# Byte-counted attention steps, flat convolution and spread state loads in a decoder trunk on one core

## The chip, the core and the metric

The kernel runs on one core of one Trainium2 chip. The metric is the device time of one execution in microseconds; lower is better. A core has TensorE (PE, with its weight loads as PEld), VectorE (DVE), ScalarE (ACT), GpSimd (POOL) and SyncE (SP), which issues nearly all transfers of this kernel.

## The reference

One inference step of a decoder layer over 256 prompt tokens and 8 x 8 sample tokens (320 columns in all), width 2048, all in float32:

```
x += 0.5 * SwiGLU_a(RMSNorm(x))            # 2048 -> 2 x 5632 -> 2048
x += TokenMix(RMSNorm(x))
x += 0.5 * SwiGLU_b(RMSNorm(x))
y  = RMSNorm(x)
```

TokenMix has one combined input projection (2048 to 11,272 columns) whose columns feed two branches. Branch A is an mLSTM with 4 heads: its q and k pass a causal convolution of width 4 over time and a SiLU; a matrix state C (256 x 256 for each head, and for each of the 8 sample sequences) is read for the sample tokens and updated. Branch B is dilated causal attention with 8 heads: the prompt attends to itself, and each sample sequence attends to 2048 old keys and values at distances 0, d, 2d, ... for three patterns, near (128 and 512 back) and far (every 16th of 2048). The branches are projected back (w_pm, w_pa), gated, added and passed through w_out. Outputs are y, the new keys and values, the new states and the last three rows before the convolution.

```
y = b + sum_i xx[:, i:i+T] * w[i]                 # causal convolution, i = 0..3
num = wgt @ v + sc * (q @ C0)                     # mLSTM, C0 of each sample sequence
C_new = sT * C0 + e * k^T v
p = softmax over old keys, new keys, three patterns; o = p @ v
```

## The kernel before

Everything hangs on one long stream of projection work on TensorE. Each weight matrix is cut into chunks of 512 x 256 numbers (512 KB). A chunk is loaded into a `raw` buffer (5 of them), rounded by ScalarE into `hi` (L236) and by VectorE into the remainder `lo = raw - hi` (L113, the call of the metered VectorE; 3 buffers each), and multiplied on TensorE (L144) in 24 matmuls of 320 columns: hi and lo of the weights against hi and lo of the activations. These results go to the PSUM tiles named `fg`. All other matmuls and transposes go to the four PSUM buffers named `bg`.

`run_job` (L282) is the planner: it walks the chunks in order, and all other work is written as Python generators that are advanced between chunks, so that their instructions lie between the matmuls of the stream. At each chunk it runs, in this order: transfers and steps that were put off by a number of chunks (`later`, `run_later`), the evacuation of the job before, the rounding of the chunk two ahead (`split_upto`), small steps put off in the same way (`soon`), then on even ticks the lists `even` and `slow`, on odd ticks the list `odd`, then the evacuations that have several steps (`every`), and last the list `fill`, as long as VectorE has room by the planner's own count (`Metered`, L103: every VectorE instruction is charged 0.16 us and 0.00104 us an element, against 3.2 us a chunk plus what extra matmuls take). At its end it loads weights as far as seven chunks ahead (`load_upto`, L202). A turn of a generator in `slow` or `odd` is thus two chunks.

Since SyncE issues all transfers in program order (`dma`, L135), a transfer that waits for a buffer or for data holds up all that stand behind it. TensorE, too, takes its instructions in program order.

The stage that matters is the combined input projection, 45 jobs. Beside it run:

- `sample_attention` (L643), in `slow`: the attention of the sample tokens to old keys and values, in 16 units of one sequence and four heads (u). It first loads near keys (`nk`) and far keys (`fk`), waits until the second job of keys is there (`M["ak"]`, L756), and starts `far_work` (L700), in `fill`: scores of the far keys on VectorE and ScalarE. Each unit takes four turns, every fourth unit five (L880): products with the old values of the unit before (`pv`, L809, tiles `vt` and `pf`) and scores of this unit; then the loads of this unit's five old-value tiles of 512 KB (`values`, L804, 5 buffers) and the next near keys, one a chunk; then probabilities.
- `combine` (L883): the transposes of four units' results, the tile `hsS`; the last one loads the attention result back as `ar`, which the branch projection w_pa needs.
- `prompt_attention` (L582), in `even`: it scales its probabilities on VectorE (L605).
- `qk_evac` (L995): the convolution. Prompt and sample columns of an evacuated projection stand in `pre` (3 columns of padding, 256 of the prompt, 8 x 11 of the samples). For each of two row blocks and four taps there are two instructions, of 256 and of 64 columns, into `y`, a tile of a ring of 19 buffers; the first tap is on ScalarE (L1018), three on VectorE; then tanh, `(tanh + 1) * y` on VectorE, and the store to `qk_d`.
- `mlstm` (L1057), in `odd`: for each head, `load_head`, `prep`, `front`, `update`, and two products of the queries with the states (`retrieve`, L1165; 16 matmuls on four tiles `C` of 256 KB). `load_c` (L1085) asks for the next four tiles at once, in five buffers. Its calls stand here (L1260 and on), a `yield` ending a turn:

```
for i in range(2):
    yield
    retrieve(h, i, CC.pop(2 * h + i))
    ...
    yield
    if i == 0:
        make_qm(h, 1)
    load_cc(2 * h + i + 1)
    ...
    yield
```

A state product is the first work of its chunk on TensorE; the matmuls of that chunk stand behind it.

Of the kernel before, what the change touches and what calls it, by code (L numbers as in the profile page):

```python
# [18 lines left out]
SEQ = 256  # L19
# [37 lines left out]
def _consts():  # L57
    c = {}
    p = np.arange(128)
    c["ident"] = np.eye(128, dtype=np.float32)  # L60
    mk = np.full((4, 4, 8, SCOLS), NEG, np.float32)
    for i in range(4):
        for t in range(8):
            mk[:, i, t, 0:128] = _logmult(512 + t - 128 * i - p)
            if i == 0:
                mk[:, i, t, 128:136] = _logmult(t - np.arange(8))
                mk[:, i, t, 136] = 0.0
            mk[:, i, t, 137] = 0.0
    mk = mk.reshape(128, SCOLS)
    c["msk_s"] = mk  # L70
    c["msk_p"] = _logmult(128 + p[:, None] - np.arange(256)[None])
    q = np.arange(32)
    bd = (p[:, None] // 32 == q[None] // 8).astype(np.float32)
    b8, t8 = np.divmod(np.arange(64), 8)
    kt_, bg_, bt_ = p // 64, (p // 32) % 2, p % 32
    sels = (bg_[:, None] * 32 + bt_[:, None] == np.arange(64)[None]).astype(np.float32)
    s4 = np.stack([np.arange(4), 3 - np.arange(4)], axis=1)
    qmask = np.tile((s4[:, :, None] == q // 8).astype(np.float32).reshape(1, 256), (128, 1))
    cm = np.full((128, 448), BIG, np.float32)
    cm[:, 0:256] = np.where(p[:, None] <= np.arange(256)[None], 0.0, BIG)  # L80
    cm[:, 256:384] = np.where(p[:, None] <= p[None], 0.0, BIG)
    s = np.arange(64)
    ok = (s[:, None] // 8 == s[None] // 8) & (s[:, None] <= s[None])
    cm[64:, 384:448] = np.where(ok, 0.0, BIG)
# [12 lines left out]


M_BD, M_SELS, M_QM, M_CM, M_TS, M_LD = 0, 32, 96, 352, 800, 832
MIXW = 833  # L100


class Metered:  # L103
# [3 lines left out]
    def __getattr__(self, name):  # L107
        fn = getattr(self.engine, name)

        def call(*a, **k):  # L110
            n = math.prod((a[1] if name == "tensor_reduce" else a[0]).shape[1:])
            self.load += 0.16 + n * (0.0066 if name == "reciprocal" else 0.00104)
            return fn(*a, **k)  # L113

        return call
# [8 lines left out]
def decoder_kernel(tc, I, O, K):  # L124
# [8 lines left out]
    es.enter_context(tc.manual_schedule())  # L133

    def dma(out, in_):  # L135
        nc.sync.dma_start(out, in_)  # L136

# [144 lines left out]
    def run_job(job):  # L282
# [4 lines left out]
        for n, (ci, k0, nk) in enumerate(cs):  # L287
            V.next_chunk(CHUNK_US + extra[0])
            extra[0] = 0.0
            run_later()  # L290
# [8 lines left out]
            if tick[0] % 2 == 0:  # L299
                step(even)  # L300
                step(slow)
            else:
# [46 lines left out]
    n0T = cp.tile([128, 64], F32, name="n0T")  # L349
    mskp = cp.tile([128, 256], F32, name="mskp")  # L350
    sTb = cp.tile([128, 32], F32, name="sTb")
# [230 lines left out]
    def prompt_attention(p):  # L582
        tb = m2_tile("tp")
        tbv = tb.rearrange("p (h c) -> p h c", h=2)
        dma(tb, I["bias_p"][p])
        G.tensor_tensor(tbv, tbv, bcast(mskp, 2), op=OP.add)
        q, k, v = QT[p], KT_[p], VP[p]
# [17 lines left out]
        def scale(m):  # L605
            s, ns = S_[m], N_[m]
            V.reciprocal(ns[:, 2:4], ns[:, 2:4])
            V.tensor_scalar(s[:, 0:128], s[:, 0:128], ns[:, 2:3], None, op0=OP.mult)
            V.tensor_scalar(s[:, 128:384], s[:, 128:384], ns[:, 3:4], None, op0=OP.mult)

# [32 lines left out]
    def sample_attention():  # L643
# [109 lines left out]
        for n in range(FKB):  # L753
            load_far(n)
            yield
        while M["ak"] < 1:  # L756
            yield
        q4 = make_q4(0)
        load_qr(0)
        yield  # L760
        load_qr(1)
        fill.append(far_work())

# [78 lines left out]
        for u in range(17):  # L842
# [23 lines left out]
            s = soft(u, sp)  # L866
            values(u, 5, 0, 1)
            later(lambda u=u: load_near(2 * u + NKB), 1)
# [4 lines left out]
            later(lambda u=u: load_near(2 * u + 1 + NKB), 1)  # L873
            values(u, 2, 3, 4)
            yield
# [3 lines left out]
            yield  # L879
            if u % 4 == 3:  # L880
                yield

# [112 lines left out]
    def qk_evac(ps, j):  # L995
# [11 lines left out]
        yield  # L1007
        y = t_tile(F32, "y")
        for m in range(2):
# [3 lines left out]
            for i in range(4):  # L1013
                w = gv[:, G_CW + 16 * i + kt:G_CW + 16 * i + kt + 1]
                for o, x in ((y[:, m, 0:SEQ], pre[:, m, i:i + SEQ]),
                             (y[:, m, SEQ:NT].rearrange("p (b t) -> p b t", b=8), pres[:, m, :, i:i + 8])):
                    if i == 0:
                        S.activation(o, x, AF.Identity, scale=w, bias=gv[:, G_CB + kt:G_CB + kt + 1])  # L1018
                    else:
                        V.scalar_tensor_tensor(o, x, w, o, op0=OP.mult, op1=OP.add)  # L1020
        yield
        e = pret[:, 0:2 * NT].rearrange("p (m c) -> p m c", m=2)
        S.activation(e, y, AF.Tanh)
        M["tanh"] = True
        yield
        V.scalar_tensor_tensor(e, e, 1.0, y, op0=OP.add, op1=OP.mult)
        if j >= 4:
# [29 lines left out]
    def mlstm():  # L1057
        mix = M["mix"]
        qmk = mix[:, M_QM:M_QM + 256].rearrange("p (a n c) -> p a n c", a=4, n=2)
        cm = mix[:, M_CM:M_CM + 448]  # L1060
        sels = mix[:, M_SELS:M_SELS + 64]
# [23 lines left out]
        def load_c(h, i):  # L1085
            c = []
            for b in (2 * i, 7 - 2 * i, 2 * i + 1, 6 - 2 * i):
                c.append(mxt([128, 512], "C", 5, "C"))
                load_state(c[-1], b, h)
            return c  # L1090

# [7 lines left out]
        def prep(h):  # L1099
            d = H[h]  # L1100
            q, k, re = d["q"], d["k"], d["re"]
            z = m2_tile("z")
            for j, (c0, c1, t0) in enumerate(((0, 256, 0), (256, 384, 128), (384, 448, 256))):
                V.scalar_tensor_tensor(z[:, c0:c1], re[:, 0, t0:t0 + c1 - c0], aeT[:, j, h:h + 1], cm[:, c0:c1],
                                       op0=OP.subtract, op1=OP.max)
# [151 lines left out]
        for h in range(4):  # L1257
            for i in range(2):
# [8 lines left out]
                if i == 1 and h < 3:  # L1267
                    while M["qk"] < 2 * (h + 2):
                        yield
                    load_head(h + 1)  # L1270
                yield
            yield
            numer(h)
# [26 lines left out]
    def mixer_open():  # L1300
# [10 lines left out]
        M["mix"] = c([128, MIXW], "mixc")  # L1311
        dma(M["mix"], K["mix"])
        M["cvn"] = c([128, 16, 27], "cvn")
        M["bif"] = c([36, 1], "bif")
# [316 lines left out]
    def init_tables():  # L1631
# [5 lines left out]
        dma(msk, K["msk_s"])  # L1637
        dma(mskp, K["msk_p"])
        dma(convst, I["conv_t"].rearrange("p (k c) -> p k c", k=16))
# [141 lines left out]
```

## Time and profile before

| | us |
|---|---|
| median of 3 runs (2677.07 to 2678.86) | 2678.45 |
| profiled execution, its own time | 2678.66 |
| its span in the profile | 2676.9 |
| TensorE busy in the span | 2652.1 |
| VectorE busy | 1516.8 |
| ScalarE busy | 1128.1 |

The granted TensorE clock is full throughout. Rows of the profile name the engine, the line of the kernel, the operation and the tiles (out<-in); a line of a helper such as L113, L136 or L144 serves many callers, so the tiles tell what it is. The list of waits says which engine sat idle for whom: total us, times, longest. The chain of waits follows back what ended last. SPq is SyncE's queue of transfers. In the timeline a row gives the start in us from the start of the span, the length in us and how many instructions were merged into it.

### The profile page before, as it was taken

Reading aid. Unit: us, or ns where it says so; the run is one execution under the profiler, and the core shown is the slowest. Engines: PE = TensorE matmul, PEld = TensorE weight load, DVE = VectorE, ACT = ScalarE, POOL = GpSimd, SP = SyncE. Lnnn points to the kernel's source line nnn. Section 1 sums busy time; section 2 is a strip of 40 time slices with the busy share of each in tenths; the row PEclk is TensorE's granted clock in tenths of the full one; section 3 lists DMA queues with packets and bytes.
Section 4 is the critical chain, followed back from the end, with each engine's and each line's share of the span. In section 5 each row is a group of like instructions: output and inputs, shape, how many; then the busy total and the mean of one; then the engine's idle time right before and its main releaser. Section 6 shows DMA issues by size and latency. Waiting matters only on the chain.

```text
span 2676.9 us, 50899 instructions
## 1 busy us (share of the span) xinstructions
PE 2652.1 (99%) x21286; PEld 2632.1 (98%) x21286; DVE 1516.8 (57%) x1994; ACT 1128.1 (42%) x1865; POOL 146.7 (5%) x167
## 2 busy tenths in 40 slices
PE   9999999999999999999999999999999999999998
PEld 9999999999999999999999999999999999999997
DVE  6444444444446577777766656655555555554445
ACT  6333333333334445555544444444333333333344
POOL 0000000000000000011211000000000000000000
PEclk9999999999999999999999999999999999999999
DMA  6554544445546779899999876665556556555543
GB/s 232 163 168 159 164 160 163 158 155 165 169 158 187 239 221 320 282 346 334 338 364 347 320 244 223 199 204 191 193 193 192 190 185 193 187 173 172 160 151 130
DMA packets 198596, 568.48 MB, mean 212 GB/s; under 512 B 23249, under 2 KB 61273, under 8 KB 198365
## 3 DMA queue, kind: packets, MB, share of 16 engines
q1 hardware_dynamic: 197644, 563.91, 63.4%
q8 instruction: 166, 2.72, 0.4%
q10 hardware_dynamic: 720, 1.31, 0.1%
q14 instruction: 66, 0.53, 0.1%
HBM read 533.41 MB, written 31.73 MB: 211 GB/s over the span
## 4 chain that ended last, share of the span: by engine, by line
PE 93%; DMA 4%; DVE 1%; ACT 1%; issue 1%; SPq 0%; DVEq 0%; ACTq 0%
PE fg L144 89%; PE bg L144 3%; DMA vt<-in_old_v_dram 2%; DVE lo L113 0%; PE bg L357 0%; ACT hi L236 0%; DMA qr<-qt_d 0%; DMA C<-in_state_C_dram 0%; DMA k<-qk_d 0%; DMA raw<-in_w_in_dram 0%; DMA fk<-in_far_k_dram 0%; SPq L136 0%; DVE x L113 0%; DMA raw<-in_w_ffa_in_dram 0%; DMA scb<-sc_d 0%
## 5 line engine op out<-in xcount | busy, mean ns | idle before, releaser
L113 DVE TENSOR_TENSOR lo<-raw,hi 128x1024 fp32r<-128x1024 f32 (+1 forms) x788 | 964.2, 1229 | 855.9 <-ACT hi L236 838.7
L144 PE MATMUL fg<-xh,hi 128*128 128x320 f32 x4232 | 1273.0, 302 | 1.7 <-ACT hi L236 0.9
L144 PE MATMUL fg<-xh,lo 128*128 128x320 f32 x4232 | 1262.2, 299 | 1.2 <-DVE lo L113 1.2
L144 PE MATMUL fg<-xl,hi 128*128 128x320 f32 x4232 | 1262.0, 299 | 0.0
L236 ACT CAST hi<-raw 128x1024 fp32r<-128x1024 f32 (+1 forms) x780 | 797.1, 1026 | 1074.7 <-PE fg L144 904.2
L144 PEld LDWEIGHTS fg<-xh,hi 128*128 128x128 f32 x4232 | 799.6, 189 | 7.3 <-issue 2.5
L144 PEld LDWEIGHTS fg<-xh,lo 128*128 128x128 f32 x4232 | 799.2, 189 | 1.7 <-DVE lo L113 1.7
L144 PEld LDWEIGHTS fg<-xl,hi 128*128 128x128 f32 x4232 | 799.4, 189 | 0.8
L144 PE MATMUL fg<-hh,hi 128*128 128x320 f32 x1408 | 421.5, 299 | 0.0
L144 PE MATMUL fg<-hh,lo 128*128 128x320 f32 x1408 | 421.1, 299 | 0.0
L144 PE MATMUL fg<-hl,hi 128*128 128x320 f32 x1408 | 421.1, 299 | 0.0
L144 PEld LDWEIGHTS fg<-hh,hi 128*128 128x128 f32 x1408 | 266.2, 189 | 0.3
L144 PEld LDWEIGHTS fg<-hl,hi 128*128 128x128 f32 x1408 | 266.2, 189 | 0.1
L144 PEld LDWEIGHTS fg<-hh,lo 128*128 128x128 f32 x1408 | 266.2, 189 | 0.0
L470 POOL TENSOR_TENSOR gt<-gt,rstd 128x640 f32<-128x640 f32 x44 | 68.1, 1547 | 1783.6 <-ACT gt L469 1783.6
L144 PE MATMUL fg<-bh,hi 128*128 128x320 f32 x512 | 153.3, 299 | 0.0
L144 PE MATMUL fg<-bh,lo 128*128 128x320 f32 x512 | 153.1, 299 | 0.0
L144 PE MATMUL fg<-bl,hi 128*128 128x320 f32 x512 | 153.1, 299 | 0.0
L144 PEld LDWEIGHTS fg<-bh,hi 128*128 128x128 f32 x512 | 96.8, 189 | 0.2 <-issue 0.2
L144 PEld LDWEIGHTS fg<-bl,hi 128*128 128x128 f32 x512 | 96.8, 189 | 0.0
L144 PEld LDWEIGHTS fg<-bh,lo 128*128 128x128 f32 x512 | 96.8, 189 | 0.0
L458 ACT CAST hh<-hf 128x640 fp32r<-128x640 f32 x44 | 34.9, 792 | 143.9 <-DVE hf L113 143.9
(253 smaller groups left out, 1358.1 us busy)
## 6 DMA issues: line engine op xcount, KB each, us to landing
raw<-in_w_in_dram SPq DMA_DIRECT2D x176, 512.0 KB
raw<-in_w_ffb_in_dram SPq DMA_DIRECT2D x176, 512.0 KB
raw<-in_w_ffa_in_dram SPq DMA_DIRECT2D x172, 512.0 KB
raw<-in_w_ffa_out_dram SPq DMA_DIRECT2D x80, 512.0 KB
vt<-in_old_v_dram SPq DMA_DIRECT2D x80, 512.0 KB
raw<-in_w_ffb_out_dram SPq DMA_DIRECT2D x80, 512.0 KB
fk<-in_far_k_dram SPq DMA_DIRECT2D x48, 512.0 KB
nk<-in_near_k_dram SPq DMA_DIRECT2D x32, 512.0 KB
```

Of the source, the lines that this page charges most:

```text
L113: return fn(*a, **k)
L144: T.matmul(out, a, b, start=start, stop=stop, **kw)
L236: S.copy(hi[:, :nk], t[:, :nk])
L458: S.copy(h, xe)
L470: G.tensor_tensor(gt, gt, bcast(rstd, 2), op=OP.mult)
```

## The change

Nine edits, all in the stage of the combined projection:

1. `dma` counts the bytes that are asked for; at each chunk the ledger `moved[1]` gains them and loses 0.38 MB for each us of the planned chunk. A step of `slow` (the sample attention) runs only while the ledger is under 3.0 MB.
2. The planner charges VectorE instructions with a scalar in their name 0.22 us instead of 0.16 us.
3. The far scheme starts when the second job of queries is there, not of keys; the first four old-value tiles are loaded in the turns between.
4. The extra turn of every fourth attention unit is gone.
5. The convolution runs over the flat row of 344 columns, prompt and samples in one instruction (the columns between samples are not used); `y` is a buffer of its own, and the product with tanh goes in three instructions to a tile `e` of the ring of 19, from which it is stored.
6. The prompt's probabilities are scaled on ScalarE.
7. The next four states are asked for one a chunk, through `later` by 1 to 4 chunks.
8. mLSTM takes one turn more behind the second state product of heads 0 to 2.
9. The mask table of mLSTM loses 128 doubled columns, and the prompt's mask table is loaded when the stage opens, into a buffer of that stage.

```diff
+    moved = [0.0, 0.0]
+    MB_PER_US = 0.38
+
     def dma(out, in_):
+        moved[0] += math.prod(out.shape) * 4e-6
         nc.sync.dma_start(out, in_)
...
-            V.next_chunk(CHUNK_US + extra[0])
-            extra[0] = 0.0
+            us = CHUNK_US + extra[0]
+            V.next_chunk(us)
+            moved[1] = max(0.0, moved[1] + moved[0] - us * MB_PER_US)
+            extra[0] = moved[0] = 0.0
             run_later()
...
                 step(even)
-                step(slow)
+                if moved[1] < 3.0:
+                    step(slow)
...
-            self.load += 0.16 + n * (0.0066 if name == "reciprocal" else 0.00104)
+            self.load += (0.22 if "scalar" in name else 0.16) + n * (0.0066 if name == "reciprocal" else 0.00104)
...
-            V.tensor_scalar(s[:, 0:128], s[:, 0:128], ns[:, 2:3], None, op0=OP.mult)
-            V.tensor_scalar(s[:, 128:384], s[:, 128:384], ns[:, 3:4], None, op0=OP.mult)
+            S.activation(s[:, 0:128], s[:, 0:128], AF.Copy, scale=ns[:, 2:3])
+            S.activation(s[:, 128:384], s[:, 128:384], AF.Copy, scale=ns[:, 3:4])
...
+        while M["aq"] < 1:
+            yield
+        load_qr(0)
+        load_qr(1)
+        fill.append(far_work())
+        for pc in range(4):
+            yield
+            load_v(0, pc)
         while M["ak"] < 1:
             yield
         q4 = make_q4(0)
-        load_qr(0)
         yield
-        load_qr(1)
-        fill.append(far_work())
...
-            if u % 4 == 3:
-                yield
...
-        y = t_tile(F32, "y")
+        y = mxt([128, 2, 344], "y", 1, "y")
...
-                for o, x in ((y[:, m, 0:SEQ], pre[:, m, i:i + SEQ]),
-                             (y[:, m, SEQ:NT].rearrange("p (b t) -> p b t", b=8), pres[:, m, :, i:i + 8])):
-                    if i == 0:
-                        S.activation(o, x, AF.Identity, scale=w, bias=gv[:, G_CB + kt:G_CB + kt + 1])
-                    else:
-                        V.scalar_tensor_tensor(o, x, w, o, op0=OP.mult, op1=OP.add)
+                o, x = y[:, m], pre[:, m, i:i + 344]
+                if i == 0:
+                    S.activation(o, x, AF.Identity, scale=w, bias=gv[:, G_CB + kt:G_CB + kt + 1])
+                else:
+                    V.scalar_tensor_tensor(o, x, w, o, op0=OP.mult, op1=OP.add)
...
+        e = t_tile(F32, "e")
...
+        V.scalar_tensor_tensor(e[:, :, 0:SEQ], th[:, :, 0:SEQ], 1.0, y[:, :, 0:SEQ], op0=OP.add, op1=OP.mult)
+        for m in range(2):
+            V.scalar_tensor_tensor(e[:, m, SEQ:NT].rearrange("p (b t) -> p b t", b=8), samples(th, m * 347), 1.0,
+                                   samples(y, m * 344), op0=OP.add, op1=OP.mult)
...
         def load_c(h, i):
             c = []
-            for b in (2 * i, 7 - 2 * i, 2 * i + 1, 6 - 2 * i):
+
+            def load(b):
                 c.append(mxt([128, 512], "C", 5, "C"))
                 load_state(c[-1], b, h)
+
+            for n, b in enumerate((2 * i, 7 - 2 * i, 2 * i + 1, 6 - 2 * i)):
+                later(lambda b=b: load(b), 1 + n)
             return c
...
                     load_head(h + 1)
                 yield
+                if i == 1 and h < 3:
+                    yield
```

More of the change, by code (lines that the diff above doesn't have):

```diff
@@ L78, in _consts @@
     qmask = np.tile((s4[:, :, None] == q // 8).astype(np.float32).reshape(1, 256), (128, 1))
-    cm = np.full((128, 448), BIG, np.float32)
+    cm = np.full((128, 320), BIG, np.float32)
     cm[:, 0:256] = np.where(p[:, None] <= np.arange(256)[None], 0.0, BIG)
-    cm[:, 256:384] = np.where(p[:, None] <= p[None], 0.0, BIG)
     s = np.arange(64)
     ok = (s[:, None] // 8 == s[None] // 8) & (s[:, None] <= s[None])
-    cm[64:, 384:448] = np.where(ok, 0.0, BIG)
+    cm[64:, 256:320] = np.where(ok, 0.0, BIG)
     klo, vlo = (p // 2 % 2).astype(np.float32), (p % 2).astype(np.float32)
@@ L96, in _consts @@
     return {k: np.ascontiguousarray(v, dtype=np.float32) for k, v in c.items()}
-M_BD, M_SELS, M_QM, M_CM, M_TS, M_LD = 0, 32, 96, 352, 800, 832
-MIXW = 833
+M_BD, M_SELS, M_QM, M_CM, M_TS, M_LD = 0, 32, 96, 352, 672, 704
+MIXW = 705
 class Metered:
@@ L349, in decoder_kernel @@
     n0T = cp.tile([128, 64], F32, name="n0T")
-    mskp = cp.tile([128, 256], F32, name="mskp")
     sTb = cp.tile([128, 32], F32, name="sTb")
@@ L585, in prompt_attention @@
         dma(tb, I["bias_p"][p])
-        G.tensor_tensor(tbv, tbv, bcast(mskp, 2), op=OP.add)
+        G.tensor_tensor(tbv, tbv, bcast(M["mskp"], 2), op=OP.add)
         q, k, v = QT[p], KT_[p], VP[p]
@@ L866, in sample_attention @@
             s = soft(u, sp)
-            values(u, 5, 0, 1)
+            values(u, *((5, 0, 1) if u else (4,)))
             later(lambda u=u: load_near(2 * u + NKB), 1)
@@ L873, in sample_attention @@
             later(lambda u=u: load_near(2 * u + 1 + NKB), 1)
-            values(u, 2, 3, 4)
+            values(u, *((2, 3, 4) if u else (5,)))
             yield
@@ L1014, in qk_evac, with samples @@
                 w = gv[:, G_CW + 16 * i + kt:G_CW + 16 * i + kt + 1]
-                for o, x in ((y[:, m, 0:SEQ], pre[:, m, i:i + SEQ]),
-                             (y[:, m, SEQ:NT].rearrange("p (b t) -> p b t", b=8), pres[:, m, :, i:i + 8])):
-                    if i == 0:
-                        S.activation(o, x, AF.Identity, scale=w, bias=gv[:, G_CB + kt:G_CB + kt + 1])
-                    else:
-                        V.scalar_tensor_tensor(o, x, w, o, op0=OP.mult, op1=OP.add)
+                o, x = y[:, m], pre[:, m, i:i + 344]
[3 more added lines that the diff above has]
+                    V.scalar_tensor_tensor(o, x, w, o, op0=OP.mult, op1=OP.add)
         yield
-        e = pret[:, 0:2 * NT].rearrange("p (m c) -> p m c", m=2)
-        S.activation(e, y, AF.Tanh)
+        th = pret[:, 0:694].rearrange("p (m c) -> p m c", m=2)
+        S.activation(th[:, :, 0:344], y, AF.Tanh)
         M["tanh"] = True
         yield
-        V.scalar_tensor_tensor(e, e, 1.0, y, op0=OP.add, op1=OP.mult)
+        e = t_tile(F32, "e")
+        def samples(t, off):
+            return raw_ap(t, 259 + off, [[t.ap[0][0], 128], [11, 8], [1, 8]])
+        V.scalar_tensor_tensor(e[:, :, 0:SEQ], th[:, :, 0:SEQ], 1.0, y[:, :, 0:SEQ], op0=OP.add, op1=OP.mult)
+        for m in range(2):
+            V.scalar_tensor_tensor(e[:, m, SEQ:NT].rearrange("p (b t) -> p b t", b=8), samples(th, m * 347), 1.0,
+                                   samples(y, m * 344), op0=OP.add, op1=OP.mult)
         if j >= 4:
@@ L1059, in mlstm @@
         qmk = mix[:, M_QM:M_QM + 256].rearrange("p (a n c) -> p a n c", a=4, n=2)
-        cm = mix[:, M_CM:M_CM + 448]
+        cm = mix[:, M_CM:M_CM + 320]
         sels = mix[:, M_SELS:M_SELS + 64]
@@ L1102, in prep @@
             z = m2_tile("z")
-            for j, (c0, c1, t0) in enumerate(((0, 256, 0), (256, 384, 128), (384, 448, 256))):
-                V.scalar_tensor_tensor(z[:, c0:c1], re[:, 0, t0:t0 + c1 - c0], aeT[:, j, h:h + 1], cm[:, c0:c1],
+            for j, (c0, t0, m0, n) in enumerate(((0, 0, 0, 256), (256, 128, 0, 128), (384, 256, 256, 64))):
+                V.scalar_tensor_tensor(z[:, c0:c0 + n], re[:, 0, t0:t0 + n], aeT[:, j, h:h + 1], cm[:, m0:m0 + n],
                                        op0=OP.subtract, op1=OP.max)
@@ L1312, in mixer_open @@
         dma(M["mix"], K["mix"])
+        M["mskp"] = mxt([128, 256], "isb", 1, "mskp")
+        dma(M["mskp"], K["msk_p"])
         M["cvn"] = c([128, 16, 27], "cvn")
@@ L1637, in init_tables @@
         dma(msk, K["msk_s"])
-        dma(mskp, K["msk_p"])
         dma(convst, I["conv_t"].rearrange("p (k c) -> p k c", k=16))
```

## The prediction

> **What bounds the kernel now.** I read the page first, then the waits of TensorE and of SyncE's queue, then busy time by stage, and last the chain of waits and the timeline around the places where TensorE stops. The page:
>
> ```profile
> span 2676.9 us, 50899 instructions
> PE 2652.1 (99%) x21286; PEld 2632.1 (98%) x21286; DVE 1516.8 (57%) x1994; ACT 1128.1 (42%) x1865; POOL 146.7 (5%) x167
> ```
>
> TensorE is busy 99% of the span, and the change neither adds nor removes a matmul. All that it can win are the stops of TensorE, and all that it can lose are new ones. The list of TensorE's waits in the stage of the change (idle us in total, times, longest):
>
> ```profile
> PE bg L144 <- DMA vt<-in_old_v_dram: 6.3, 5, 2.0
> PE bg L144 <- DVE hsS L113: 2.0, 1, 2.0
> PE fg L144 <- DVE lo L113: 1.2, 2, 0.7
> PE fg L144 <- ACT hi L236: 0.9, 1, 0.9
> ```
>
> Together 10.4 us, of which old-value tiles that land late make 6.3 us. Where they lie shows in the windows (length; busy us of PE, PEld, DVE, ACT, POOL; granted clock; share of the DMA engines; GB/s):
>
> ```profile
> 1040.00:1140.00 100.00, 98.42 (x949) 97.28 (x948) 76.63 (x168) 54.51 (x158) 7.21 (x15) 1.00 0.86 302
> 1140.00:1240.00 100.00, 94.59 (x1031) 90.81 (x1030) 72.19 (x161) 52.60 (x163) 16.54 (x34) 1.00 0.97 348
> 1240.00:1340.00 100.00, 98.04 (x944) 94.73 (x943) 78.17 (x174) 59.50 (x160) 20.50 (x30) 1.00 0.96 333
> 1340.00:1440.00 100.00, 99.07 (x1072) 95.27 (x1071) 68.53 (x142) 47.40 (x155) 14.29 (x17) 1.00 1.00 361
> ```
>
> The clock is full, and TensorE is short of work by 1.6, 5.4, 2.0 and 0.9 us where the DMA engines are nearly full. So the stage is bound by TensorE, with a transfer system that has no room left. The chain of waits gives the price of one transfer there (start, us from issue to the end of what it held up):
>
> ```profile
> 1125.77 5.99 DMA raw<-in_w_in_dram
> 1131.78 3.97 DMA scb<-sc_d
> 1161.19 5.81 DMA fk<-in_far_k_dram
> 1168.81 11.23 DMA vt<-in_old_v_dram
> 1201.79 8.79 DMA qr<-qt_d
> 1210.60 6.98 DMA k<-qk_d
> 1354.17 7.77 DMA C<-in_state_C_dram
> ```
>
> A tile asked for less than about 7 us before its use will stop TensorE; one asked for 11 us before will not, or hardly.
>
> **The ledger and the removed turns.** An attention step now waits while the ledger of asked-for bytes stands at 3.0 MB or more. The ledger pays off 0.38 MB per us of planned TensorE time, 1.22 MB in a plain chunk of 3.2 us. Sizes:
>
> ```profile
> vt<-in_old_v_dram SPq DMA_DIRECT2D x80, 512.0 KB
> C<-in_state_C_dram SPq DMA_DIRECT2D x32, 256.0 KB
> ```
>
> The worst chunk of before asks for four attention tiles and one weight tile of 512 KB, four states of 256 KB, and mLSTM's q, k and rows: some 5.1 MB, of which 3.9 MB stay over. Walking the issues in their order in the code with these sizes, the ledger holds back about six attention steps of the some seventy. Held attention lets the queue empty, and the late old-value tiles are a queue of about 11 us against about three chunks between request and use. A chunk and an attention step on TensorE:
>
> ```profile
> 1400.68 3.26 PE fg L144 x24
> 1416.41 3.51 PE bg L144 x134
> ```
>
> Three chunks are 9.8 us. With 3 MB or less outstanding, at the 361 GB/s of the fourth window, the queue is about 8.3 us long, less than those 9.8 us. I take all 6.3 us as won; at worst none.
>
> Six held turns cost attention 6 x 2 x 3.26 = 39 us of its schedule; the removed extra turn at every fourth step returns 4 x 2 x 3.26 = 26 us, and the earlier far scheme about one turn. What then is late? Attention ends with these:
>
> ```profile
> L144 PE MATMUL bg<-vt,pf x768: 272/273/298, 1037.3 to 1590.4; 128*32 128x128 f32 x192
> 1610.22 1.96 SPq L136 DMA_DIRECT2D ar<-ha_d  x4
> L458 ACT CAST bh<-ar x4: 795/808/817, 1637.8 to 1639.9; 128x640 fp32r<-128x640 f32 x4
> ```
>
> Its result is loaded back at 1610.2 us and first needed at 1637.8 us: 27 us of cover against a delay of some 13 us less the far scheme's turn. I cost the delay at nothing; with the cover gone (two held turns more, and a landing) it would be up to 10 us.
>
> The far scheme starts when the queries are there, about one turn earlier. It asks for four 512 KB tiles early, ahead of the first product with old values at 1037.3 us (the row above). Cost: nothing.
>
> **The flat convolution and the scaling.** Durations (mean ns second to last before the bar):
>
> ```profile
> L113 DVE SCALAR_TENSOR_TENSOR y<-pre,gv,y 128x256 f32<-128x256 f32 x48 | 24.3, 507 | 4.6 <-ACT y L1018 4.6
> L113 DVE SCALAR_TENSOR_TENSOR y<-pre,gv,y 128x64 f32<-128x64 f32 x48 | 13.3, 277 | 0.0
> L113 DVE SCALAR_TENSOR_TENSOR pre<-pre,y 128x640 f32<-128x640 f32 x8 | 6.5, 816 | 0.0
> L113 DVE TENSOR_SCALAR s<-s,ns 128x256 f32<-128x256 f32 x8 | 2.8, 348 | 0.0
> ```
>
> A job goes from 6 x (507 + 277) = 4.70 us to six operations of 344 columns. These lie between 507 and 784 ns; on the line through the two rows, 1.2 ns a column, 612 ns: 3.67 us, a saving of 1.0 us. The product of 816 ns becomes three, which adds up to 0.5 us. Net 0.5 us a job on VectorE, 4 us over eight jobs, on an engine that is 69 to 78% busy and for which TensorE waits 1.2 us in the whole run. The scaling moves at most 16 x 0.35 = 5.6 us from VectorE to ScalarE, which is 47 to 60% busy; it may add a ScalarE wait for the reciprocal, behind which the next weight rounding queues, with two split chunks as cover. On the path: 0, between -2.1 us (all waits on lo and hi go) and +2.1 us (they double). The product now sits in a buffer of the 19-slot ring until its store has landed; a late slot would stop VectorE, and the same two chunks cover it. Smaller masks and the table's later load: nothing.
>
> **The states, one a chunk.** This is the term that decides. The load of the next four C tiles is called one turn (two chunks) after the first product of a head with its states. The second product comes two turns, four chunks, after that call. Before, all four requests went out at the call:
>
> ```profile
> 1440.02 3.99 SPq L136 DMA_DIRECT2D C<-in_state_C_dram  x4
> 1452.76 1.07 PE L144 MATMUL bg<-C,qm 128*32 128x256 f32 x16
> ```
>
> The last is issued by 1444.0 us, 8.7 us ahead of the product, and TensorE waits for no C tile anywhere. Now the requests are put off by 1, 2, 3 and 4 chunks: the fourth is issued at the start of the very chunk whose product needs it. How far SyncE is ahead of TensorE at that place shows in the first transfer of the same chunk, for this product and the same one of the other three heads:
>
> ```profile
> 1452.25 0.42 SPq L136 DMA_DIRECT2D fk<-in_far_k_dram  x1
> 1191.06 1.06 SPq L136 DMA_DIRECT2D vn<-vs_d  x1
> 1194.09 1.07 PE L144 MATMUL bg<-C,qm 128*32 128x256 f32 x16
> 1281.59 0.43 SPq L136 DMA_DIRECT2D fk<-in_far_k_dram  x1
> 1281.32 1.07 PE L144 MATMUL bg<-C,qm 128*32 128x256 f32 x16
> 1371.12 0.33 SPq L136 DMA_DIRECT2D vt<-in_old_v_dram  x1
> 1368.22 1.07 PE L144 MATMUL bg<-C,qm 128*32 128x256 f32 x16
> SPq L136 <- DVE lo L113: 1809.3, 681, 9.1
> ```
>
> Issue minus product: -0.51, -3.03, +0.27, +2.90 us, mean -0.09. SyncE can't run further ahead: each weight load waits for the rounding of a chunk in whose buffer it lands (the last row), and the C request is queued behind that. So the fourth tile is asked for when TensorE is there. TensorE can do 12 of the 16 products first, 12/16 x 1.07 = 0.80 us, and then stops; every matmul of the projection is queued behind it. I price the landing at the mean of the six rows of the chain that are not old values, (5.99 + 3.97 + 5.81 + 8.79 + 6.98 + 7.77) / 6 = 6.55 us: one stop is 6.55 - 0.09 - 0.80 = 5.7 us, four heads 22.6 us. Lower end, the 3.97 us row: 3.1 us each, 12.3 us. Upper end, the 11.23 us row: 10.3 us each, 41.4 us.
>
> By the Trainium skill (DMA: Bandwidth & Descriptors, Anatomy of one DMA) a transfer costs about 2.0 us and its bytes at 436 GB/s, so 256 KB land in an estimated 2.6 us, and the four stops would come to an estimated 7 us. No row of this stage is that quick: a transfer of a quarter of the size took 3.97 us.
>
> mLSTM's extra turn moves later heads two chunks on each. The 2.0 us stop on hsS is an attention transpose one chunk ahead of a state update for the same PSUM buffers; the two move apart. I take the 2.0 us as gone (0 to 2.0).
>
> **The sum.** The profiled execution took 2678.66 us, 1.8 us round its span of 2676.9 us, and the median is 2678.45 us, 0.2 us less, so I leave it out. 2678.66 - 6.3 - 2.0 + 22.6 = 2693.0 us.
>
> **The rivals.**
> (a) The states land in time, and the change is faster. This needs an attention step (3.51 us on TensorE) in the chunk ahead of each second product, as ahead of the row at 1194.09, where SyncE was 3.03 us early, and a landing at the 3.97 us end: 3.97 - 3.03 - 0.80 = 0.1 us each. Then 2678.66 - 6.3 - 2.0 = 2670.4 us. It decides from a request 7 us ahead. For it: the held queue is shorter. Against: one row in four has that order, and the removed turns shift it.
> (b) The held queue lands the states quickly, so that gain and loss cancel: 3.97 us a tile, with an attention step ahead of two of the four: 2678.66 - 8.3 + 2 x 3.1 = 2676.6 us, no change. By the fixed price of the Trainium skill (above) it would come out about the same. Against it is every other row of the chain.
> (c) The ledger doesn't do what it says: it pays off 380 GB/s where the fullest window moved 361, so the queue is longer than the ledger thinks and the old values stay late: 2678.66 + 22.6 = 2701.3 us, or more with the upper price.
> (d) Attention is held past its 27 us of cover: up to 10 us on top, 2703 us.
>
> **How the numbers follow.** The forecast has 0.53, (a) 0.15, (b) 0.12, (c) 0.15, (d) 0.05. A difference under 0.2%, 5.4 us, can't be told from none here. Slower is the forecast, (c) and (d), 0.73; same 0.12; faster 0.15. The lower bound leaves out most of (a): 2674 us takes in (b). The upper: the dear end of the states with the gains kept, 2678.66 - 8.3 + 41.4 = 2711.8, 2712 us.
>
> **What would show it.** Right: TensorE's waits list C from in_state_C, four times, 3 to 10 us each, and old values no more; the C requests stand singly between weight loads, the last beside its product; TensorE's busy time falls short by some 5 us around four places where mLSTM's state products lie. The VectorE row of y has 344 columns and near 612 ns. Wrong: no wait on C, or one under 2 us each; old values still in the list; a wait on the attention result (ar) near the end of the output gates; a longer wait on lo or hi.

## The result and the profile after

The changed kernel takes 2715.94 us in the median, against 2678.65 us for the kernel before on the same chip: a ratio of 1.0136, interval 1.0123 to 1.015. One execution of 4680.45 us, with a granted clock of 0.555, stands outside the comparison. The profiled execution took 2714.77 us, 36.1 us more than that of before. The forecast was 2693.0 us with a range up to 2712: right in direction, and less than half of the loss.

The page of the kernel after. TensorE's instructions are the same in number, but its busy time is 12.8 us longer, which no added work explains:

```profile
span 2713.0 us, 50853 instructions
PE 2664.9 (98%) x21286; PEld 2638.0 (97%) x21286; DVE 1514.1 (56%) x1946; ACT 1131.7 (42%) x1865; POOL 148.4 (5%) x167
```

TensorE's waits in the kernel after (total us, times, longest):

```profile
PE bg L147 <- DMA C<-in_state_C_dram: 31.9, 11, 8.1
PE fg L147 <- issue: 1.7, 2, 1.0
PE fg L147 <- ACT hi L1607: 1.2, 2, 0.9
PE fg L147 <- DVE lo L112: 0.3, 1, 0.3
```

The waits on `vt` (6.3 us) and on `hsS` (2.0 us) are gone, as forecast. In their place stands one wait, on the states, of 31.9 us. It lies at the second product of each head. Head 1 is the worst; first SyncE's requests for its third and fourth tile, then the product's 16 matmuls (start, length; in brackets the wait ahead):

```profile
1290.64 0.51 SPq L139 DMA_DIRECT2D C<-in_state_C_dram  x1
...
1295.83 0.38 SPq L139 DMA_DIRECT2D C<-in_state_C_dram  x1
```

```profile
1291.30 1.39 PE L147 MATMUL bg<-C,qm 128*32 128x256 f32 x8
1300.76 1.06 PE L147 MATMUL bg<-C,qm 128*32 128x256 f32 x2 [8.07 <-DMA C<-in_state_C_dram]
1305.26 1.07 PE L147 MATMUL bg<-C,qm 128*32 128x256 f32 x6 [3.44 <-DMA C<-in_state_C_dram]
```

TensorE came at 1291.30 us. The third tile had been asked for only 0.7 us earlier, the fourth was asked for 4.53 us later. Both stops are simply those landings. The fourth landings of the four heads stand in the chain of waits (request, us until it landed); the row at 1390.14 us is the first tile of head 2:

```profile
1191.82 5.60 DMA C<-in_state_C_dram
...
1295.83 9.39 DMA C<-in_state_C_dram
...
1390.14 9.04 DMA C<-in_state_C_dram
1399.24 7.80 DMA C<-in_state_C_dram
...
1499.81 7.41 DMA C<-in_state_C_dram
```

And where TensorE was in the other three heads:

```profile
1188.01 0.64 PE L147 MATMUL bg<-C,qm 128*32 128x256 f32 x8
...
1399.31 0.59 PE L147 MATMUL bg<-C,qm 128*32 128x256 f32 x2 [2.22 <-DMA C<-in_state_C_dram]
...
1499.96 0.62 PE L147 MATMUL bg<-C,qm 128*32 128x256 f32 x2
```

The fourth request went out 3.81, 4.53, 2.15 (TensorE came at 1399.31 - 2.22) and -0.15 us behind TensorE's coming, 2.6 us in the mean, and landed in 7.55 us in the mean. At head 2 TensorE already stopped for the first tile, though that had been asked for 7 us ahead: it took 9.04 us to land.

The second loss shows in the windows (length; busy us of PE, PEld, DVE, ACT, POOL; granted clock; DMA share; GB/s), of the kernel after: the whole stretch with the states, and three pieces of head 1, from the product's start on:

```profile
1160.00:1520.00 360.00, 327.01 (x3209) 309.19 (x3207) 223.85 (x443) 160.99 (x460) 45.03 (x69) 0.94 0.84 297
...
1291.30:1295.50 4.20, 1.25 (x9) 0.28 (x8) 3.50 (x12) 1.33 (x3) 1.55 (x4) 1.00 1.03 414
1295.60:1309.00 13.40, 4.80 (x18) 3.11 (x19) 0.00 (x0) 0.37 (x1) 0.00 (x0) 0.50 0.88 308
1309.10:1316.00 6.90, 6.90 (x52) 6.90 (x52) 3.39 (x5) 3.34 (x5) 0.00 (x0) 1.00 0.23 73
```

The same stretch in the kernel before:

```profile
1160.00:1520.00 360.00, 353.73 (x3616) 341.93 (x3615) 261.91 (x556) 191.92 (x580) 50.01 (x71) 1.00 0.96 342
```

For the first 4.2 us, of which TensorE works 1.25, the clock is still full. Then it is 0.50 for 13.4 us and outlasts the stop, which ends at 1305.26 us; only then is it full again. The last row also shows the transfers behind a stop: a DMA share of 0.23 and 73 GB/s, where the stop itself had 1.03 and 0.88.

The convolution and the end of attention, in the kernel after (groups by form, then the rows of the tile `ar`):

```profile
L112 DVE SCALAR_TENSOR_TENSOR y<-pre,gv,y 128x344 f32<-128x344 f32 x48 | 27.6, 575 | 6.8 <-ACT y L1025 5.7
L112 DVE SCALAR_TENSOR_TENSOR e<-pre,y 128x512 f32<-128x512 f32 x8 | 5.5, 693 | 0.0
L112 DVE SCALAR_TENSOR_TENSOR e<-pre,y 128x64 f32<-128x64 f32 x16 | 4.8, 340 | 0.0
```

```profile
L139 SPq DMA_DIRECT2D ar<-ha_d x4: 427/464/1185, 1660.4 to 1662.7; - x4
L463 ACT CAST bh<-ar x4: 797/802/809, 1674.7 to 1676.9; 128x640 fp32r<-128x640 f32 x4
```

### The profile page after: what moved, and what is told of

It reads as the page before. It is cut to its first block, busy times and chain, and to the rows that moved or that the text cites. A ratio compares the mean times of both kernels' runs of the same rounds, so it can differ in the third digit from the quotient of the medians.

```text
span 2713.0 us, 50853 instructions
## 1 busy us (share of the span) xinstructions
PE 2664.9 (98%) x21286; PEld 2638.0 (97%) x21286; DVE 1514.1 (56%) x1946; ACT 1131.7 (42%) x1865; POOL 148.4 (5%) x167
## 4 chain that ended last, share of the span: by engine, by line
PE 96%; DMA 2%; DVE 1%; ACT 0%; issue 0%; SPq 0%; DVEq 0%; ACTq 0%
PE fg L147 91%; PE bg L147 4%; DMA C<-in_state_C_dram 1%; PE bg L362 1%; DMA fk<-in_far_k_dram 0%; DMA raw<-in_w_in_dram 0%; DVE lo L112 0%; DMA x<-in_x_t_dram 0%; DVE x L112 0%; ACT hi L239 0%; SPq L139 0%; DVE fk L112 0%; DVE rows L112 0%; DVE sm L112 0%; ACT xh L1617 0%
```

## The experiments

The theory after the result: the loss is edit 7 alone, and it has two terms, the stops themselves and a TensorE at half clock behind them. The rivals: another edit (held attention, convolution, scaling) slows the stage; or the stops are all, and the slow clock costs nothing.

**1. All of the change, but the states asked for at once.**

```diff
-                later(lambda b=b: load(b), 1 + n)
+                load(b)
```

> The changed kernel with one edit undone: the four state tiles are again asked for at the call. Theory (the fourth tile is asked for at its use, and the stop also halves the clock for a while): TensorE's waits on C go from 31.9 us to under 1 us, the mean granted clock from 0.991 back to 0.998, and since the waits on old values (6.3 us) and on hsS (2.0 us) stay away, the time is 2666 to 2673 us, some 45 us under the changed kernel. Rival 1 (the held attention steps or the extra mLSTM turns cost the time, and C only happens to be what ends last): 2695 us or more, another wait in C's place. Rival 2 (spreading the states is what removed the waits on old values): waits on vt of 4 us or more come back, 2675 us or more.

Measured: 2672.31 us, ratio to before 0.9981 (0.9972 to 0.9991). TensorE's waits in this kernel, beside two of 1.1 and 1.0 us that are the same in all:

```profile
PE fg L147 <- DVE lo L112: 2.5, 3, 1.5
PE fg L147 <- ACT hi L1607: 1.4, 1, 1.4
PE bg L147 <- issue: 1.2, 1, 1.2
...
PE bg L147 <- POOL re L1230: 0.8, 2, 0.5
PE fg L147 <- issue: 0.6, 1, 0.6
```

No C, no `vt`, no `hsS`. Edit 7 alone turns a small gain into the loss. The gain is 5.4 us against the kernel before on the same chip (2677.75 us). The two profiled spans differ by 2713.0 - 2670.4 = 42.6 us, and their waits by (31.9 + 1.7 + 1.2 + 0.3) - (2.5 + 1.4 + 1.2 + 0.8 + 0.6) = 28.6 us. So 14.0 us of the loss are no wait at all: TensorE is busy that much longer with the same instructions.

**2. The spread alone, on the kernel before.** Edit 7's lines, nothing else.

> The kernel before with one edit alone: the four state tiles are asked for one a chunk, by 1 to 4 chunks after the call. Theory: waits on C of 25 to 40 us and a mean granted clock of 0.990 to 0.993; the old values come less late, since each stop lets the queue empty: 2705 to 2720 us. Rival (the spread is harmless without the other edits): within 5 us of the kernel before, no wait on C over 1 us.

Measured: 2707.57 us, ratio 1.0105 (1.0088 to 1.0122). Its waits and its window:

```profile
PE bg L144 <- DMA C<-in_state_C_dram: 23.7, 8, 6.0
PE bg L144 <- DVE hsS L113: 2.0, 1, 2.0
```

```profile
1160.00:1520.00 360.00, 334.31 (x3275) 318.52 (x3275) 235.55 (x502) 174.67 (x525) 45.64 (x69) 0.95 0.89 313
```

The C wait is a little under what was expected, and close to the 22.6 us of the prediction; the low clock is here too. The `vt` waits are gone without any ledger; that the old values catch up while TensorE stands is likely, but no run shows it, and the kernel before with edits 7 and 8 (run 8) keeps 3.4 us of them. So their absence in the kernel after doesn't show by itself that the ledger works.

**3. The call for the states one turn (two chunks) earlier**, still one a chunk:

```diff
                 retrieve(h, i, CC.pop(2 * h + i))
+                load_cc(2 * h + i + 1)
...
-                load_cc(2 * h + i + 1)
```

> The changed kernel with the call for the next states one turn (two chunks) earlier, right behind the state product; they are still asked for one a chunk. The fourth is then asked for 6.5 us of TensorE work earlier. In the changed kernel the fourth request to its landing took 5.6 to 9.4 us, and it was issued 0.2 us before to 4.5 us after the product's start. Theory: stops of 0 to 4 us a head, 0 to 12 us in all, the clock at 0.996 or more: 2670 to 2685 us. Rival (the number of separate requests is what costs, not when they are made): waits on C stay above 20 us, 2705 us or more.

Measured: 2676.65 us, ratio 0.999 (0.9981 to 1.0), within what was expected.

```profile
PE bg L147 <- DMA C<-in_state_C_dram: 5.4, 2, 2.8
```

Spreading by itself is not the fault; asking too late is. Two chunks of lead remove 26.5 of 31.9 us, and 4.3 us are left against the states at once (2672.31 us on the same chip). What is left are two waits of 2.81 and 2.58 us at one head, with 0.62 us of work between, and even these are followed by half clock (a window from inside the second wait on, columns as above):

```profile
1378.40:1385.00 6.60, 5.25 (x22) 4.44 (x23) 0.00 (x0) 0.37 (x1) 0.00 (x0) 0.50 0.99 395
```

**4. The fourth request one chunk earlier**, with the third:

```diff
-                later(lambda b=b: load(b), 1 + n)
+                later(lambda b=b: load(b), min(1 + n, 3))
```

> The kernel after, with the states asked for 1, 2, 3 and 3 chunks behind the call instead of 1, 2, 3 and 4: the fourth request a chunk of 3.2 us earlier, everything else as in after. Theory (the stop is the fourth landing less its lead, and the half clock follows only stops over some 3 us): each stop falls by about 3.2 us, idle on C from 31.9 to about 19 us, half-clock stretches fewer or shorter, and the time falls by 13 us and a part of the 12 to 16 us of the slow clock, to 2692 to 2702 us. Rival 1 (the queue sets the landing: an earlier request lands no earlier, since the transfers share one full set of engines): the idle on C stays at 28 to 35 us and the time at 2712 to 2718 us. Rival 2 (any stop halves the clock for the same stretch, whatever its length): 13 us less and the slow clock as before, 2702 to 2705 us.

Measured: 2703.72 us, ratio 1.0094 (1.0079 to 1.0109).

```profile
PE bg L147 <- DMA C<-in_state_C_dram: 23.2, 8, 8.2
```

The wait fell by 8.7 us, not 13: the third tile is late as well and stays so, and the fourth now lands behind it. The time lies in the second rival's range, though not by that rival's sum, which had 13 us less of waits and the slow clock as before: TensorE's busy time fell by 2.4 us as well (2664.9 to 2662.6), so the slow clock became a little cheaper. How its length follows the length of a stop is not settled by this run; the rival that an earlier request lands no earlier falls.

**5. and 6. The stops filled with work.** Matmuls of a table of ones, whose results nobody uses, ahead of the second product: 64 a head, and 20 a head.

```diff
+            if i == 1:
+                ps = bg_tile()
+                for _ in range(64):
+                    T.matmul(ps[:, 0:128], ones, ones, start=True, stop=True)
```

> The changed kernel with 64 matmuls of the table of ones (128 x 128, about 7 us, result unused) ahead of the second state product of each head, where TensorE stands waiting. The wait for C itself is not shortened. Theory (the stop costs twice: the idle time, and then about 10 us at half clock): the half-clock stretches go or shorten, the mean granted clock rises to 0.995 or more, and the time falls by 4 to 11 us to 2704 to 2711 us, although TensorE has more work. Rival (the clock does not matter, only the idle time): within 2 us of the changed kernel or slower by up to 5 us, where a stop is shorter than the filler.

> The kernel after, with 20 matmuls of ones (128 columns, into a free PSUM tile) ahead of each head's second state product, so that TensorE works through the first part of each stop. The filler of the kernel with 64 of them took 57.8 us for four heads of 64, 0.226 us a matmul; 20 take 4.5 us a head, 18 us in all, less than each of the four stops of after (8.2, 11.5, 7.2 and 4.9 us). Theory (the stops cost twice: the idle time, and a TensorE at half clock behind them): the work stream stands just as long, but the idle rest is 31.9 - 18 = about 14 us in pieces of 0.4 to 7 us, most half-clock stretches go, and the time falls from 2715.9 to 2702 to 2710 us. Rival 1 (only the idle time counts; slow stretches come from elsewhere): 2713 to 2718 us, with the half-clock stretches still there. Rival 2 (the filler displaces the loads' landing, each stop gets longer by it): 2720 us and over.

Measured with 64: 2725.7 us (1.0176, 1.0161 to 1.0191). The group of the filler, the waits and the window:

```profile
L1192 PE MATMUL bg<-ones 128*128 128x128 f32 x512 | 57.8, 275 | 0.0
```

```profile
PE fg L147 <- issue: 2.1, 2, 1.7
...
PE fg L147 <- ACT hi L1611: 0.9, 1, 0.9
PE fg L147 <- DVE lo L112: 0.3, 1, 0.3
```

```profile
1160.00:1520.00 360.00, 359.57 (x3540) 349.86 (x3540) 219.63 (x428) 159.30 (x458) 43.57 (x68) 1.00 0.82 294
```

Each filler matmul takes two records, and the group took twice what was expected, so the time that had been forecast for this run was missed. Yet the sum tells the price of the clock. Filler for waits should have made the span longer by 57.8 - 31.8 = 26.0 us (the waits on other engines differ by 0.1); it grew by 10.3 us, 2713.0 to 2723.3. So 15.7 us came back with the full clock.

Measured with 20: 2710.18 us (1.0118, 1.0103 to 1.0133): more work on TensorE than in the kernel after, and faster, though the two intervals overlap at their ends.

```profile
PE bg L147 <- DMA C<-in_state_C_dram: 16.7, 6, 4.3
PE fg L147 <- ACT hi L1611: 1.7, 1, 1.7
...
PE fg L147 <- DVE lo L112: 0.3, 1, 0.3
```

```profile
L1192 PE MATMUL bg<-ones 128*128 128x128 f32 x160 | 18.5, 275 | 0.0
```

```profile
1160.00:1520.00 360.00, 343.32 (x3399) 329.52 (x3398) 225.51 (x445) 163.65 (x465) 45.31 (x69) 0.97 0.84 298
```

The waits fell by 35.1 - 18.7 = 16.4 us and 18.5 us of filler came in, +2.1 us; the span went down by 4.9 us, 2713.0 to 2708.1. Half of the lost clock (0.94 to 0.97) is thus worth 7.0 us, and all of it an estimated 14.0, as coarse as these two digits. The rival that only idle time counts falls. Runs 1, 5 and 6 put the term at 14.0, 15.7 and 14.0 us.

**7. and 8. Why the stops grew from 23.7 to 31.9 us: edit 8, mLSTM's extra turn.** The kernel after without it, and the kernel before with edits 7 and 8.

```diff
-                if i == 1 and h < 3:
-                    yield
```

> The kernel after without edit 8 alone (mLSTM's extra turn behind heads 0 to 2); the states still come one a chunk. In after the fourth request of a head went out 3.81 and 4.53 us behind the product's start, then 0.07 and 0.15 us ahead of it (mean +2.03); with the spread alone on the kernel before it was -2.19, +0.27, +3.70, -0.46 (mean +0.33) and TensorE waited 23.7 us for C instead of 31.9. Theory (edit 8 moves the state products against the attention steps, so that SyncE stands later): the mean goes back under +1 us, the waits on C to 22 to 27 us, and the time from 2715.9 to 2700 to 2708 us. Rival 1 (the held and removed attention turns moved them): the mean stays near +2 us, C at 29 to 34 us; the time is 2709 to 2715 us, since the extra turn alone cost 3.4 us with the states at once. Rival 2 (it is chance from head to head): any of the two sums, with other heads late than before.

> The kernel before with edits 7 and 8 alone: states one a chunk, and mLSTM's extra turn. The spread alone ran 2707.6 us with 23.7 us of waits on C. Theory (edit 8 moves the state products to where SyncE stands later): C waits of 28 to 36 us and 2711 to 2720 us. Rival 1 (the held and removed attention turns moved them): C waits of 20 to 27 us and 2703 to 2711 us.

Measured: 2701.12 us (1.0075, 1.006 to 1.009) without it, 2716.07 us (1.013, 1.0113 to 1.0147) with edits 7 and 8 alone. The wait on C in the kernel after without edit 8:

```profile
PE bg L147 <- DMA C<-in_state_C_dram: 20.8, 6, 5.4
```

and in the kernel before with edits 7 and 8:

```profile
PE bg L144 <- DMA C<-in_state_C_dram: 26.9, 10, 8.2
PE bg L144 <- DMA vt<-in_old_v_dram: 3.4, 2, 2.6
```

Fourth request against TensorE's coming, by the timeline of each kernel as above:

| kernel | four heads, us | mean | wait on C |
|---|---|---|---|
| after | 3.81, 4.53, 2.15, -0.15 | 2.59 | 31.9 |
| before with 7 and 8 | -2.19, 5.91, 2.84, -0.54 | 1.50 | 26.9 |
| before with 7 | -2.19, 0.27, 3.70, -0.46 | 0.33 | 23.7 |
| after without 8 | 3.80, -4.25, 0.62, -4.24 | -1.02 | 20.8 |

The wait follows the mean, 11.1 us for 3.61 us over four heads. Edit 8 moves the mean later in both kernels, but by 1.2 us in the one and 3.6 us in the other, and single heads jump by several us either way. That edit 8 makes the stops longer in these two kernels is shown; that it does so by one fixed amount is not. The run with 7 and 8 has its wait on C in the rival's range and its time in the theory's; the wait on `vt` makes part of the difference. It takes as long as the whole change (2715.94 us).

**9. Without edit 8, states at once.** Run 1 without the extra turn.

> The kernel with all of the change but the spread states (2672.3 us), and without edit 8, mLSTM's extra turn behind heads 0 to 2. Theory (the prediction's step: the turn moves a state update away from an attention transpose for the same PSUM buffers): a wait of TensorE on hsS of about 2 us, or one like it on a bg tile, comes back, and the time is 2673 to 2676 us. Rival (the two have moved apart by the other edits, the held and the removed attention turns, and the extra turn does nothing): no such wait, 2671 to 2673.5 us.

Measured: 2668.45 us, ratio 0.9966 (0.9954 to 0.9979).

```profile
PE bg L147 <- DVE hsS L112: 0.8, 1, 0.8
```

Neither theory had this: the extra turn costs some 3.4 us (against 2671.87 us for run 1's kernel on the same chip) and saves at most the 0.8 us of this wait. Where the 3.4 us arise stays open.

**10. The convolution, the scaling, the planner's charge and the tables alone** (edits 2, 5, 6 and 9 on the kernel before).

> The kernel before with the flat convolution, the scaling on ScalarE, the planner's new charge and the smaller tables alone (edits 2, 5, 6 and 9); no ledger, old far scheme, all attention turns, states at once, mLSTM as before. Theory (the prediction's step: VectorE has room, so the path sees nothing of it): within 2.1 us of before, 2676 to 2680 us, with vt and hsS waits as in before. Rival 1 (the rounding of lo and hi was what TensorE lacked): lo and hi waits gone and the time 2673 to 2676 us. Rival 2 (the planner's dearer charge lets less far work in a chunk and the far scheme comes late): waits on tiles of attention and 2681 us or more.

Measured: 2675.68 us, ratio 0.9994 (0.9985 to 1.0003): nothing that can be told from no change, the median 0.3 us under the expected range. That is in the first rival's range, but the waits on lo and hi, which that rival has gone, are still 1.0 and 1.3 us. Its profile has one new wait of 2.8 us, on attention's `fr`, and only 1.0 us on `vt` and 0.8 on `hsS`, with no edit that was meant for them.

**11. The ledger alone** (edit 1 on the kernel before).

> The kernel before, with the ledger alone (edit 1): attention steps are held while it stands at 3.0 MB or more. Theory (the ledger lets the old values land in time): the 6.3 us of vt waits go, hsS keeps its 2.0 us or moves, and the time is 2670 to 2675 us against 2678. Rival 1 (the ledger doesn't bite, it pays off faster than the queue moves): vt waits stay at 4 to 8 us, 2676 to 2680 us. Rival 2 (held back without the removed turns, attention ends late): the vt waits go but TensorE waits for ar up to 20 us near the end of the stage, 2680 to 2695 us.

Measured: 2687.04 us, ratio 1.0034 (1.0021 to 1.0047), rival 2 in its lower half. The longest wait, and the tile `ar`:

```profile
PE fg L148 <- ACT bh L465: 5.1, 1, 5.1
```

```profile
L140 SPq DMA_DIRECT2D ar<-ha_d x4: 359/472/500, 1642.8 to 1644.8; - x4
L465 ACT CAST bh<-ar x4: 763/774/791, 1646.3 to 1649.7; 128x640 fp32r<-128x640 f32 x4
```

The `vt` waits are gone, but the attention result is asked for at 1642.8 us and used 3.5 us later, where before there were 27 us between. The wait of 5.1 us is not all: TensorE's busy time is 6.1 us longer than before (2658.2 against 2652.1), with a mean clock of 0.996 instead of 0.998. Held attention has a price, and edits 3 and 4 together pay it (run 13); what each pays, no run tells.

**12. Run 1's kernel without the ledger** (its limit set out of reach), twice, the second time beside run 1's kernel on one chip.

```diff
-                if moved[1] < 3.0:
+                if moved[1] < 1e9:
```

> The kernel with all of the change but the spread states (2672.3 us), and the ledger's limit set so high that no attention step is held back. Theory (the prediction's step on the ledger: it lets the old values land in time): waits on vt come back, 3 to 8 us in all, and the time is 2675 to 2680 us. Rival (the old values are in time because of the removed turns, the earlier far scheme and the moved heads, not because of the ledger): no vt wait, 2671 to 2674 us.

> The kernel with all of the change but the spread states once more, beside the same without the ledger on one chip, in five rounds. Theory (the ledger keeps the old values in time, by 3 to 4 us in the median): 2671 to 2674 us, under before by 0.15 to 0.25%, and under the one without the ledger by 2 to 5 us. Rival (the difference between the two was a difference of chips): the same as without the ledger to 1 us.

> The kernel with all of the change but the spread states and the ledger. Theory (without the ledger the landing of the old values is left to chance from execution to execution): 2674 to 2678 us in the median, with a spread of 5 us or more between executions, against 2 us with the ledger. Rival (the ledger does nothing here): the same as with the ledger, 2671 to 2674 us, and as steady.

Measured: 2676.3 us (0.9991, 0.9982 to 1.0001) the first time; then 2675.93 us (0.9993, 0.9985 to 1.0002) against 2671.87 us (0.9979, 0.997 to 0.9988) with the ledger. Executions spread from 2671.93 to 2679.42 us and from 2673.24 to 2679.63 without it, from 2670.37 to 2674.23 with it (and from 2671.35 to 2676.66 in run 1). The first profile without it:

```profile
PE bg L147 <- DMA vt<-in_old_v_dram: 2.8, 2, 1.6
```

The old values come late again, by less than in the kernel before. The ledger is worth about 4 us in the median, and steadier executions.

**13. The attention edits alone** (1, 3 and 4 on the kernel before).

> The kernel before with edits 1, 3 and 4 alone (ledger, earlier far scheme, no extra turn of attention); convolution, scaling, planner's charge, states and mLSTM as before. With the other edits but 7 and 8 as well it ran 2668.5 us, the ledger alone 2687.0 us, where TensorE waited 5.1 us for the attention result at the stage's end. Theory (the removed turns pay for the held ones, and the gain of the whole comes from the attention side): no vt wait, no bh wait, 2667 to 2672 us. Rival (the gain needs the shorter convolution and the scaling on ScalarE as well): 2673 to 2679 us, with waits on lo, hi or attention tiles.

Measured: 2667.12 us, ratio 0.9953 (0.9938 to 0.9968), the lowest of all, though its interval overlaps that of run 9. Its window has no idle TensorE at all:

```profile
1160.00:1520.00 360.00, 360.00 (x3675) 349.82 (x3674) 256.86 (x533) 186.16 (x534) 49.19 (x71) 1.00 0.95 342
```

No other edit adds a gain that can be measured: the gain of the change lies in these three; `hsS` has no wait here, with no extra turn of mLSTM.

## Why the prediction was wrong in size

**The step that failed: "The states, one a chunk".** The forecast took one stop as 6.55 (landing) - 0.09 (SyncE's lead) - 0.80 (products done first) = 5.7 us, four of them 22.6 us. The mechanism and the place were right, and so was the tile, though it wasn't the only late one. On the kernel before, whose timeline gave the numbers, it came to 23.7 us (run 2). That this is so close is in part luck: the fourth tiles landed there in 7.0 us in the mean, not 6.55, and SyncE stood at +0.33 us, not -0.09, which makes 26.2 us, and products in pieces covered more than 0.80 us a head. The stops were mis-sized in the kernel after, and a term was missing.

*SyncE's lead was taken from a timetable that the change itself moved.* The four leads of before (-0.51, -3.03, +0.27, +2.90) had a spread of 6 us, and I used their mean. Edit 8 was in the same list of edits and moved the products: in the kernel after the mean was +2.59 us and the landing 7.55 us, so the same sum gives 4 x (7.55 + 2.59 - 0.80) = 37.4 us where 31.9 was measured. Of the difference to 22.6 the lead makes 10.7 us and the landing 4.0. The 5.5 us less come from the products: cut into pieces by the waits, and in part at half clock, they covered more than 0.80 us, at head 1 1.39 + 1.06 us. (Ten of the 16 stand ahead of the fourth tile, x8 and x2 in the timeline, not twelve as the prediction counted.) Also, the third tile was late at every head, and at head 2 all four were, which the forecast left out. The upper price of 41.4 us held these waits; the value in the middle did not.

*A term was missing: the clock.* A stop was priced as idle time only. The runs put 14 to 16 us on top, for a clock that is halved during the stop and stays so behind it. The Trainium skill (TensorE: Matmul & The Clock Gate, Part 1 and Why this matters for your kernels) says that TensorE falls back to half rate after an idle window of about 3.4 us, and warns of gaps over about 3 us. The trace agrees in the main: no wait of before exceeded 2.0 us and its stretch stands at 1.00, the four stops of after are 4.9 to 11.5 us and it stands at 0.94. But less was enough here than the 3.4 us: the waits of 2.81 and 2.58 us of run 3 were followed by half clock, and so was the single wait of 2.8 us on `fr` in run 10, with 0.54 over the next 3.3 us. The forecast had the 5.7 us stops and never set them beside that rule; with 14 us more it would have been 2707 us.

The balance: -6.3 (`vt`) - 2.0 (`hsS`) + 31.9 (C) + 0.3 (issue, hi and lo together) + 14 (clock) = 37.9 us, against 36.1 measured between the profiled executions. The 14 us are against run 1; with the 12.8 us by which TensorE is busy longer than before, the sum is 36.7.

**The ledger.** Its -6.3 us came. All eleven profiles with the ledger have no wait on `vt`; of the six without it five have one, of 1.0 to 6.3 us, and run 2 has none. So the ledger does what it says, though in the kernel after the stops may have done a part of it. In the version without stops it is worth about 4 us (run 12). Rival (c), a ledger that doesn't bite, falls with run 11.

**Held attention.** Costed at nothing, and nothing it was: `ar` is asked for at 1660.4 us and wanted at 1674.7, so of 27 us of cover 14 are left, a delay of 13 us as forecast. Rival (d) fell for the whole change, but it is real for the ledger alone (run 11): the returned turns were a needed part of the sum, as the prediction had it.

**The `hsS` wait.** It went, and the turn that the prediction credited can do it: run 2 has the 2.0 us, and with edit 8 added (run 8) they are gone. But the turn isn't needed: run 13 and the kernel after without edit 8 (run 7) have neither the turn nor the wait, and run 9 has 0.8 us. And the turn costs 3.4 us with the states at once (run 9) and, with the spread states, about 15 (2701.12 against 2715.94 us). A gain of 2.0 us was put down to an edit that cost more than that in both settings.

**Convolution and scaling.** Right: 575 ns for 344 columns against an estimate of 612. A job has 6 x 575 = 3.45 us instead of 4.70, and its product 693 + 2 x 340 = 1373 ns instead of 816; net 0.7 us saved against 0.5 forecast, and nothing of it on the path (run 10).

**Rivals (a) and (b).** States that land in time would have given 2670.4 us; they did not, but run 1, where they do, gives 2672.31. Rival (b) falls: the quickest of the fourth tiles took 5.60 us in a stretch with a DMA share of 0.84. The estimate of 2.6 us a landing is not met either. The section of the Trainium skill that it was worked out from (DMA: Bandwidth & Descriptors, Anatomy of one DMA) gives its fit for transfers issued by GpSimd; these are issued by SyncE, so the runs don't test the fit itself.

## What to carry to other kernels

When an edit puts requests off, compare each with where the issuing engine stands relative to its user, take the late end of that spread rather than its mean, and read it from a timetable in which the change's other edits have been moved too. Price a stop of TensorE of several us twice, once as idle time and once as half clock behind it (here 14 us beside 31.9). When a list of edits loses as a whole, take them one at a time: three of these nine made the kernel 0.5% faster, and two spoiled it.

## What the runs showed of the hardware

The granted clock was 1.00 or 0.50 in the pieces shown, and at head 1 the half lasted 13.4 us, of which TensorE was busy 4.80 us. So the price is not half of all the low time: 0.06 of 360 us is an estimated 21.6 us of full clock lost, and the kernel paid 14 to 16 of them, because the rest fell into the stop itself. Waits of 2.6 to 2.8 us were enough for the half clock in runs 3 and 10. And a stop can be cheaper filled than empty: 18.5 us of useless matmuls made the kernel about 5 us faster (the span by 4.9 us, 2713.0 to 2708.1).
